# The first norm's sums from the transposed input, and the compressed branch projected first, in a hybrid decoder layer

## The chip, the cores and the metric

One core of one Trainium2 chip runs the whole layer. The metric is the device time of one execution in microseconds (us), lower is better. A profile is one further execution with the hardware profiler on; its times stand beside the plain ones.

## What is computed

One decoder layer over x, 1024 positions by 1024 channels, float32. Only the head of it matters here:

```
h  = x * rsqrt(mean(x*x, channels) + 1e-6) * norm1_g
hp = h @ w_in            # S5 channels, queries, keys and values, branch gates, merge gates
kc, vc = compress_blocks(part of hp)      # blocks of 32 positions through a small MLP
y  = merge(s5(hp), sparse_attention(hp, kc, vc))
x  = x + y @ w_out;  x = x + relu(rmsnorm(x) @ w_up)**2 @ w_down
```

The scale of the norm is one number for each position, so it can be applied behind the projection: the kernel projects x times norm1_g and multiplies the results by `rstd`, the 1024 values of rsqrt.

## The kernel before

**Layout.** x comes in transposed (`xT`, 128 channels by 1024 positions for each of eight k). Each float32 operand is split into a high part (ScalarE, ACT) and a low part (VectorE, DVE, or GpSimd, POOL), and each product is three matmuls (`mm3`, lines 76 to 78). `hTh` and `hTl` are the parts of x times norm1_g for the eight k and stay for the whole projection stage.

**u projection (lines 193 to 206).** For each k the program loads a slice of x and a block of the S5 weights `wu`, splits both, and runs 24 matmuls of 512 columns (8 x 24 = 192) into eight PSUM banks: `u0` and `u1` in the pool of two large buffers, `u2a` to `u3b` in the four small ones.

**Norm (lines 208 to 221).** In the same loop the program loads x a second time, now with positions on the partitions (sixteen tiles `xt` of 128x512), squares them on ACT with a running sum into `ss2`, and behind the loop adds the two halves and takes rsqrt in some ten small DVE steps into `rstd`. Then five DMAs in a chain, each waiting for the one before it: `rstd` goes to memory (`rD`), comes back over all partitions (`rbc`), is permuted in memory (`rsD`), repeated (`rbD`) and loaded as `rU`, the scale in the order of the S5 scan.

**Behind it.** The u banks are copied out by ACT and DVE into `uT` (two buffers) and stored to `uD`; the S5 batches load `Uc` from there and POOL multiplies it by `rU`. The token projections (`proj_tok`, tiles `pj`, 24 matmuls of 268 columns for each of eight tiles) are evicted by ACT with `rstd` (`rw`) and by DVE (`gl`). The compressed projection (`proj_cmp`, tiles `ck`, 48 matmuls of 512 columns for each of two) is evicted by DVE times `rbc` into `cT`, stored, and starts the compressed branch. The list in line 684 sets the order: `wkv0`, then the compressed `wc`, `wq0`, `wkv1`. An S5 batch runs beside them as a generator: its matrices `O1` need the powers `Pr`, `Pi` that POOL builds in a chain of small steps, and its matmuls `kp` need `AB`, which POOL adds.

**What sets the order.** A scheduler places every instruction when the program is built; on the chip each engine then runs its own list in that order, and an instruction that waits holds up all behind it. All DMAs are issued by one queue (SP). Weights pass through two raw buffers, so a third load waits until POOL or DVE has split the first.

Of the kernel before, what the change touches and what calls it, by code (L numbers as in the profile page):

```python
# [8 lines left out]
F32 = mybir.dt.float32  # L9
F32R = mybir.dt.float32r  # L10
I32 = mybir.dt.int32
AF = mybir.ActivationFunctionType
ALU = mybir.AluOpType
# [4 lines left out]
EPS = 1e-6  # L18
# [20 lines left out]
def hybrid_block(ctx: ExitStack, tc: tile.TileContext, A, out):  # L39
    nc = tc.nc  # L40
    PE, ACT, DVE, POOL, SP = nc.tensor, nc.scalar, nc.vector, nc.gpsimd, nc.sync
# [38 lines left out]
    def tt(e, o, a, b, op):  # L80
        e.tensor_tensor(out=o, in0=a, in1=b, op=op)  # L81
# [4 lines left out]
    def ts(e, o, a, s1, op0, s2=None, op1=None):  # L86
        if op1 is None:
            e.tensor_scalar(out=o, in0=a, scalar1=s1, scalar2=None, op0=op0)
        else:
            e.tensor_scalar(out=o, in0=a, scalar1=s1, scalar2=s2, op0=op0, op1=op1)  # L90
# [4 lines left out]
    def act(o, i, func=AF.Copy, **kw):  # L95
        ACT.activation(out=o, in_=i, func=func, **kw)  # L96
# [29 lines left out]
    cA = pool("cA", caas, side="right")  # L126
# [49 lines left out]
    def xtile(name):  # L176
        return xp.tile([128, 1024], F32, tag="xs", name=name)
# [4 lines left out]
    s5 = pool("s5", s5es, bufs=2)  # L182
# [6 lines left out]

    HALVES = [slice(0, 512), slice(512, 1024)]  # L190
    ss = cA.tile([128, 8], F32, name="ss")
    ss2 = cA.tile([128, 2, 8], F32, name="ss2")
    for k in range(8):
        xs = xtile("xs")
        if k:
            wh, wl = W.get("wu", A["wu"][k], DVE)
        for sl in HALVES if k == 0 else [slice(0, 1024)]:
            tc.keep_in_program_order(SP.dma_start(out=xs[:, sl], in_=A["xT"][k * 128:(k + 1) * 128, sl]))
            split_scaled(hTh[k][:, sl], hTl[k][:, sl], xs[:, sl], g1[:, k:k + 1])
            if k + sl.start == 0:  # L200
                wh, wl = W.get("wu", A["wu"][k], DVE, NP0)
        for half, m in ([(h, m) for h in range(2) for m in (2, 3, 0, 1)] if k == 0 else [(h, m) for m in (2, 3, 0, 1) for h in range(2)]):
                ms = slice(m * 128, (m + 1) * 128)
                mm3(ubank(m, half), wh[:, ms], wl[:, ms],
                    hTh[k][:, HALVES[half]], hTl[k][:, HALVES[half]], k == 0, k == 7)
        if k == 7:
            break
        for t in ((0, 1) if k == 0 else (k + 1,)):
            for hf, sl in enumerate(HALVES):
                xt = s5.tile([128, 512], F32, tag=("Ct", "St")[hf], name="xt")  # L210
                SP.dma_start(out=xt, in_=A["x"][t * 128:(t + 1) * 128, sl])
                act(xt, xt, AF.Square, accum_out=ss2[:, hf, t:t + 1])
    with tc.high_priority():
        tt(DVE, ss, ss2[:, 0], ss2[:, 1], ALU.add)
        ts(DVE, ss, ss, 1.0 / 1024, ALU.mult, EPS, ALU.add)
        rsqrt(cA, rstd, ss[:], "r1")
        SP.dma_start(out=rD[:].rearrange("(t p) -> p t", p=128), in_=rstd, allow_slow_non_contiguous=True)
        SP.dma_start(out=rbc, in_=rD[:].partition_broadcast(128))
        SP.dma_start(out=rsD[:], in_=rD[:].rearrange("(k s) -> s k", s=8), allow_slow_non_contiguous=True)
        SP.dma_start(out=rbD[:], in_=rsD[:].unsqueeze(1).to_broadcast([8, 16, 128]))  # L220
        SP.dma_start(out=rU, in_=rbD[:].rearrange("s c k -> (s c) k"))
# [139 lines left out]
    def wblock(name):  # L361
        return [W.get(name, A[name][j]) for j in range(4)]
# [317 lines left out]

    for _ in range(3):
        next(active[0])
    wa = wblock("wkv0")
    for nm, g, c0 in (("wc", 0, 256), ("wq0", None, None), ("wkv1", 0, 0), ("wm", 1, 256)):
        wn = None
        for st in proj_cmp(wa) if g is None else proj_tok(wa, g, c0):
            wn = wn or (wblock(nm) if nm != "wm" else gate_weights(0))
            bg(st)
        wa = wn
        if (g, c0) == (0, 0):  # L690
            act(gl, gl, AF.Tanh, scale=0.5)
            ts(DVE, gates, gl, 0.5, ALU.mult, 0.5, ALU.add)
            scales(0, cA, Parts(xtile("sc")))
# [3 lines left out]
    wa = wlast.pop()  # L697
# [324 lines left out]
    def T_tile(name):  # L1022
        return tmp.tile([128, 1024], F32, tag="t", bufs=3, name=name)
# [103 lines left out]
    for first_k, ms in ((0, ((0, 4, 1, 5), (0, 4, 1, 5))), (2, ((2, 6, 3, 7), (2, 3, 6, 7)))):  # L1127
        ws = {}
        for hf, order_ in zip((1, 0), ms):
            sl = HALVES[hf]  # L1130
# [39 lines left out]
    for i in range(4):  # L1170
        r = [T_tile("wo") for _ in range(2)]
# [6 lines left out]
        for c, hf in ((0, 0), (0, 1), (1, 1), (1, 0)):  # L1178
            o, sl = X2[i + 4 * c], HALVES[hf]
# [12 lines left out]
    r = [T_tile("rr") for _ in range(2)]  # L1192
# [111 lines left out]
    for j in range(1, NG - 1):  # L1304
        up(j)
        if j == 6:
            acc = {}
            for q, mo, hf in (("11", 0, 0), ("22", 4, 1), ("3", 0, 1), ("4", 4, 0)):
                acc[q] = [mlp.tile([128, 1024], F32, name=f"acc{q}{i}") for i in range(2)]
                for i in range(2):  # L1310
                    SP.dma_start(out=acc[q][i][:].rearrange("p (a t) -> p a t", a=2),
                                 in_=xD[mo + 2 * i:mo + 2 * i + 2].rearrange("a p t -> p a t")[:, :, HALVES[hf]])
# [14 lines left out]
    for p in range(7 * len(groups)):  # L1327
        g, n = groups[p // 7], ORDER[p % 7]
# [12 lines left out]
        if last and n in ("B21", "B22", "T4"):  # L1341
            a = acc[TO[n][0]]
            mo, hf = {"B21": (0, 0), "B22": (0, 1), "T4": (4, 0)}[n]
# [24 lines left out]
def layouts(inp):  # L1368
    f = {k: np.asarray(v) for k, v in inp.items()}
    x = f["x"][0]  # L1370
    w = f["w_in"][0]
    r = {}
    r["x"] = x
    r["xT"] = x.T
    r["g1"] = f["norm1_g"][0].reshape(8, 128).T

    def kblocks(cols, per):
        n = cols.shape[1]
        return cols.reshape(8 // per, per, 128, n).transpose(0, 2, 1, 3)

    perm = np.arange(512).reshape(4, 8, 16).transpose(0, 2, 1).reshape(512)
    r["wu"] = w[:, 0:512][:, perm].reshape(8, 128, 512)

    def kv(b, v, g):
        c = 1024 + ((b * 2 + v) * 2 + g) * 64
        return w[:, c:c + 64]

    gcol = w[:, 1792:1816]
    for g in range(2):
        q = w[:, 512 + g * 256:768 + g * 256]  # L1390
        kvg = np.concatenate([kv(1, 0, g), kv(2, 0, g), kv(1, 1, g), kv(2, 1, g)], axis=1)
        if g == 0:
            q = np.concatenate([q, gcol[:, :12]], axis=1)
            kvg = np.concatenate([kvg, gcol[:, 12:]], axis=1)
        r[f"wq{g}"] = kblocks(q, 2)
        r[f"wkv{g}"] = kblocks(kvg, 2)
    r["wc"] = kblocks(w[:, 1024:1280], 2)

    def dup(a):
        a = a.T  # L1400
        return np.concatenate([a, a], axis=0)

    r["a_re"] = dup(f["ssm_a_re"][0])
    r["a_im"] = dup(f["ssm_a_im"][0])
    r["log_dt"] = np.broadcast_to(f["ssm_log_dt"][0], (128, 32))
    br, bi = (f[n][0].transpose(1, 0, 2) for n in ("ssm_b_re", "ssm_b_im"))
    cr, ci = (f[n][0].transpose(2, 0, 1) for n in ("ssm_c_re", "ssm_c_im"))
    cat = lambda a, b: np.concatenate([a, b], axis=0)
    r["b1"], r["b2"], r["c1"], r["c2"] = cat(br, bi), cat(bi, br), cat(cr, ci), cat(ci, cr)
    r["dsk"] = np.broadcast_to(f["ssm_d"][0].reshape(32, 16), (16, 32, 16))  # L1410
    f32 = np.float32
    sg = np.ones((128, 2), f32)
    sg[64:, 0] = -1
    sg[:64, 1] = -1
    r["sgn"] = sg
    r["kidx"] = np.broadcast_to(np.arange(128, dtype=f32), (128, 128))
    r["gq"] = np.concatenate([f["q_norm_g"][0]] * 2)[:, None]
    r["gk"] = np.concatenate([f["k_norm_g"][0].T] * 2, axis=0)
    for c in "kv":
        r["w1" + c] = f[f"cmp_w{c}1"][0].reshape(16, 128, 128).transpose(1, 0, 2)  # L1420
        r["w2" + c] = f[f"cmp_w{c}2"][0]
        r["pe" + c] = f[f"cmp_pe_{c}"][0].reshape(16, 128).T
    p = np.arange(128)[:, None]
    d = p + 896 - np.arange(1024)[None]
    r["cbias"] = np.where(d >= 0, -d, NEG).astype(f32)
    d = p + 512 - np.arange(640)[None]
    r["wbias"] = np.where((d >= 0) & (d < 512), -d, NEG).astype(f32)
    d = p + 865 - 16 * np.arange(120)[None]
    r["mbias"] = np.where(d >= 0, -d, NEG).astype(f32)
    r["cval"] = (p >= 31).astype(f32)  # L1430
    hs = np.ones((2, 6), f32)
    for h in range(8):
        hs[h // 4, h % 4] = 0.125 / SLOPES[h]
    r["hsc"] = np.broadcast_to(hs, (128, 2, 6))
    r["bglu"] = f["ssm_b_glu"][0][perm].reshape(4, 128).T
    def mblocks(a):
        nk, nm = a.shape[0] // 128, a.shape[1] // 128
        return a.reshape(nk, 128, nm, 128).transpose(2, 1, 0, 3)

    r["wglu"] = mblocks(f["ssm_w_glu"][0][perm][:, perm])  # L1440
    r["wps"], r["wpn"] = mblocks(f["w_proj_ssm"][0][perm]), mblocks(f["w_proj_nsa"][0])
    r["wm"] = mblocks(w[:, 1816:])
    r["wo"] = mblocks(f["w_out"][0])
    r["wup"] = mblocks(f["w_up"][0])
    r["wdn"] = f["w_down"][0]
    r["g2"] = f["norm2_g"][0].reshape(8, 128).T
    r["ident"] = np.eye(128, dtype=f32)
    return {k: np.ascontiguousarray(v) for k, v in r.items()}
# [19 lines left out]
```

## Time and profile before

| | us |
|---|---|
| median of three runs | 1604.04 (1601.93 to 1607.71) |
| the profiled execution | 1599.55 |
| its span, first to last instruction | 1597.5 |
| TensorE busy | 1470.0 (92%) |
| VectorE busy | 1215.1 (76%) |
| GpSimd busy | 1031.2 (65%) |
| ScalarE busy | 706.3 (44%) |
| load of x a second time | 16 DMAs of 256 KB |

TensorE is near full over the whole span. A busy share is a mean over stages; the stage that the change touches is the first 240 us, and there its idle time lies in a few long gaps.

### The profile page before, as it was taken

How to read it: one execution, taken by the hardware profiler on the slowest of the kernel's cores; microseconds unless marked ns; L12 is line 12 of the kernel's file. 1: busy time of each engine (PE TensorE's matmuls, PEld its weight loads, DVE VectorE, ACT ScalarE, POOL GpSimd, SP SyncE). 2: the span in 40 equal slices, each digit the busy share in tenths (PEclk: the TensorE clock that was granted, in tenths of full speed). 3: DMA queues.
4: the chain of work that ended last, by engine and by line, in shares of the span. 5: the costliest groups of instructions: out<-in, count | busy, mean ns of one | idle time of the engine just before them, and what ended most of it. 6: DMA issues, size and time to landing. Idle time of an engine off the chain costs nothing.

```text
span 1597.5 us, 21469 instructions
## 1 busy us (share of the span) xinstructions
PE 1470.0 (92%) x7174; PEld 1218.0 (76%) x7174; DVE 1215.1 (76%) x1833; ACT 706.3 (44%) x1443; POOL 1031.2 (65%) x875
## 2 busy tenths in 40 slices
PE   8599899999988999998788868999999889999999
PEld 6488788788977888887566756888888667787877
DVE  6366887521278878976798998977778999998965
ACT  6143433321277878887545542222222244343431
POOL 2565466442055546553688967988888766989883
PEclk9799999999989999999898979999999989999999
DMA  8654523352211111112935225332232341323202
GB/s 283 87 158 117 152 83 106 106 182 93 76 34 45 59 57 53 37 54 72 356 106 185 92 86 192 139 112 106 106 111 92 107 144 67 132 82 125 77 1 105
DMA packets 111680, 174.86 MB, mean 109 GB/s; under 512 B 23489, under 2 KB 44737, under 8 KB 111570
## 3 DMA queue, kind: packets, MB, share of 16 engines
q1 hardware_dynamic: 111570, 173.49, 33.4%
q8 instruction: 57, 0.93, 0.2%
q14 instruction: 53, 0.43, 0.1%
HBM read 125.20 MB, written 46.22 MB: 107 GB/s over the span
## 4 chain that ended last, share of the span: by engine, by line
PE 30%; DVE 12%; DMA 4%; POOL 3%; issue 3%; ACT 0%; SPq 0%; DVEq 0%; POOLq 0%; ACTq 0%
PE wT L76 3%; PE wT L77 3%; PE wT L78 3%; PE wB L76 2%; PE wB L78 2%; PE wB L77 2%; PE dn L78 2%; PE dn L76 2%; PE dn L77 2%; POOL wl L81 2%; DVE rr L81 2%; PE dnc L76 1%; PE dnb L78 1%; PE dnc L77 1%; PE dnc L78 1%
## 5 line engine op out<-in xcount | busy, mean ns | idle before, releaser
L81 POOL TENSOR_TENSOR wl<-raw,wh 128x512 fp32r<-128x512 f32 x132 | 196.7, 1500 | 85.8 <-ACT wh L96 85.5
L81 POOL TENSOR_TENSOR wl<-wd,wh 128x512 fp32r<-128x512 f32 x96 | 147.2, 1542 | 61.6 <-ACT wh L96 61.2
L96 ACT ACTIVATE wh<-raw 128x512 fp32r<-128x512 f32 x132 | 82.2, 628 | 159.8 <-PE wB L77 81.4
L90 POOL TENSOR_SCALAR pS<-pS,rs 128x128 f32<-128x128 f32 (+7 forms) x64 | 48.2, 754 | 105.6 <-DVE rs L81 69.0
L96 ACT ACTIVATE wh<-wd 128x512 fp32r<-128x512 f32 x96 | 59.2, 625 | 103.6 <-POOL wd L81 41.7
L81 DVE TENSOR_TENSOR pl<-ptp,ph 128x512 fp32r<-128x512 f32 x132 | 88.3, 686 | 18.6 <-ACT ph L96 17.4
L76 PE MATMUL gt<-hTh,wmh 128*128 128x512 f32 x256 | 101.6, 397 | 0.0
L77 PE MATMUL gt<-hTl,wmh 128*128 128x512 f32 x256 | 101.3, 396 | 0.0
L78 PE MATMUL gt<-hTh,wml 128*128 128x512 f32 x256 | 101.2, 395 | 0.0
L81 POOL TENSOR_TENSOR wl<-sum,wh 128x512 fp32r<-128x512 f32 x56 | 89.3, 1597 | 17.6 <-ACT wh L96 17.6
L96 ACT ACTIVATE ph<-ptp 128x512 fp32r<-128x512 f32 (+1 forms) x148 | 83.9, 589 | 13.7 <-PE ptp L898 11.8
L81 DVE TENSOR_TENSOR rr<-rr,rs 128x512 f32<-128x512 f32 x64 | 88.3, 1388 | 1.8
L81 POOL TENSOR_TENSOR wd<-wd 128x512 f32<-128x512 f32 x48 | 76.6, 1600 | 2.9 <-PE dnb L77 1.0
L96 ACT ACTIVATE wh<-sum 128x512 fp32r<-128x512 f32 x56 | 35.1, 628 | 92.3 <-PE wT L77 29.5
L81 DVE TENSOR_TENSOR rr<-wT,rr 128x512 f32<-128x512 f32 x80 | 54.7, 686 | 27.3 <-PE wT L78 26.7
L81 DVE TENSOR_TENSOR gt<-gt,rbc 128x512 f32<-128x512 f32 x32 | 22.0, 688 | 68.3 <-PE gt L78 61.7
L93 DVE SCALAR_TENSOR_TENSOR rr<-rr 128x512 f32<-128x512 f32 x64 | 70.5, 1107 | 1.8
L96 ACT ACTIVATE pW<-pW,mx 128x64 f32<-128x64 f32 (+5 forms) x128 | 65.4, 515 | 7.2 <-DVE mx L853 6.7
L90 POOL TENSOR_SCALAR pW<-pW,rs 128x64 f32<-128x64 f32 (+5 forms) x128 | 67.2, 538 | 0.0
L889 PE MATMUL op<-ph,vs 128*128 128x512 f32 x132 | 61.2, 464 | 2.0 <-DVE ot L81 1.4
L853 DVE CUSTOM_DVE_ANT_0 pS<-sS,c_cbias 128x128 f32<-128x128 f32 (+7 forms) x64 | 48.1, 752 | 19.5 <-PE sS L819 16.4
L81 POOL TENSOR_TENSOR wml<-wmr,wmh 128x512 fp32r<-128x512 f32 x32 | 43.5, 1364 | 25.8 <-ACT wmh L96 25.6
(638 smaller groups left out, 5233.7 us busy)
## 6 DMA issues: line engine op xcount, KB each, us to landing
raw<-in_wup SPq DMA_DIRECT2D x68, 256.0 KB, 2.6
wd<-in_wdn SPq DMA_DIRECT2D x64, 256.0 KB, 2.9
hD<-rr SPq DMA_DIRECT2D x26, 512.0 KB, 2.7
ru<-hD SPq DMA_DIRECT2D x18, 512.0 KB, 3.9
wmr<-in_wm SPq DMA_DIRECT2D x32, 256.0 KB, 2.9
gD<-gt SPq DMA_DIRECT2D x32, 256.0 KB, 2.1
g<-gD SPq DMA_DIRECT2D x32, 256.0 KB, 5.4
raw<-in_wo SPq DMA_DIRECT2D x20, 256.0 KB, 3.3
```

The source lines that it names most:

```text
L76: PE.matmul(out=o, lhsT=lh, rhs=rh, start=first, stop=False)
L77: PE.matmul(out=o, lhsT=lh, rhs=rl, start=False, stop=False)
L78: PE.matmul(out=o, lhsT=ll, rhs=rh, start=False, stop=last)
L81: e.tensor_tensor(out=o, in0=a, in1=b, op=op)
L90: e.tensor_scalar(out=o, in0=a, scalar1=s1, scalar2=s2, op0=op0, op1=op1)
L93: DVE.scalar_tensor_tensor(out=o, in0=a, scalar=s, in1=b, op0=op0, op1=op1)
L96: ACT.activation(out=o, in_=i, func=func, **kw)
L853: DVE.tensor_tensor_reduce(out=dst, in0=ps, in1=bias, scale=nsl, scalar=3e38, op0=ALU.add, op1=ALU.min, accum_out=mx[:, b, h:h + 1])
L889: PE.matmul(out=op, lhsT=vv, rhs=ph, start=n == 0, stop=n == len(jobs) - 1)
```

## The change

The second load of x goes, with its squares and `ss2`. In its place ACT squares the halves of the slices of x that are there already, POOL adds them up over k into `ssqT` and `ssqUc` (128 channels by 512 positions each; 14 additions), and behind the loop eight matmuls of one column with a column of ones sum over the partitions into a PSUM tile `ssp`, position on the partition, from which DVE takes the mean. The compressed projection moves to the head of the list, ahead of `wkv0`.

```diff
@@ u projection and norm
-    ss2 = cA.tile([128, 2, 8], F32, name="ss2")
+    ssq = [s5.tile([128, 512], F32, tag=t, name="ssq" + t) for t in ("T", "Uc")]
+    one = cA.tile([128, 1], F32, name="one")
+    DVE.memset(one, 1.0)
...
-        if k == 7:
-            break
-        for t in ((0, 1) if k == 0 else (k + 1,)):
-            for hf, sl in enumerate(HALVES):
+        for hf, sl in enumerate(HALVES):
+            if k == 0:
+                act(ssq[hf], xs[:, sl], AF.Square)
+            else:
                 xt = s5.tile([128, 512], F32, tag=("Ct", "St")[hf], name="xt")
-                SP.dma_start(out=xt, in_=A["x"][t * 128:(t + 1) * 128, sl])
-                act(xt, xt, AF.Square, accum_out=ss2[:, hf, t:t + 1])
+                act(xt, xs[:, sl], AF.Square)
+                tt(POOL, ssq[hf], ssq[hf], xt, ALU.add)
     with tc.high_priority():
-        tt(DVE, ss, ss2[:, 0], ss2[:, 1], ALU.add)
-        ts(DVE, ss, ss, 1.0 / 1024, ALU.mult, EPS, ALU.add)
+        sps = B_tile("ssp", (128, 8))
+        for t in range(8):
+            PE.matmul(out=sps[:, t:t + 1], lhsT=ssq[t // 4][:, t % 4 * 128:(t % 4 + 1) * 128], rhs=one, start=True, stop=True)
+        ts(DVE, ss, sps, 1.0 / 1024, ALU.mult, EPS, ALU.add)
@@ order of the projections
-    wa = wblock("wkv0")
-    for nm, g, c0 in (("wc", 0, 256), ("wq0", None, None), ("wkv1", 0, 0), ("wm", 1, 256)):
+    wa = wblock("wc")
+    for nm, g, c0 in (("wkv0", None, None), ("wq0", 0, 256), ("wkv1", 0, 0), ("wm", 1, 256)):
```

The scheduler places everything anew up to the middle of the attention. The list of the DMA queue SP before, from the last slice of x on (out<-in, partitions by elements; `wcr`, `wkv0r` and `wq0r` are raw weights):

```order
L198 DMA xs<-in_xT 128x1024
L142 DMA wkv0r<-in_wkv 128x536 x3
L217 DMA rD<-rstd 128x8x1
L142 DMA wkv0r<-in_wkv 128x536
L218 DMA rbc<-rD 128x1024
L219 DMA rsD<-rD 1024x1x1
L357 DMA uD<-uT 128x8x128
L220 DMA rbD<-rsD 128x1x128
L142 DMA wcr<-in_wc 128x512
L357 DMA uD<-uT 128x8x128
L142 DMA wcr<-in_wc 128x512
L221 DMA rU<-rbD 128x128
```

And the same queue in the changed kernel, from the weights that follow the last slice of x:

```order
L142 DMA wcr<-in_wc 128x512 x4
L142 DMA wkv0r<-in_wkv 128x536 x4
L361 DMA uD<-uT 128x8x128
L142 DMA wq0r<-in_wq 128x536
L361 DMA uD<-uT 128x8x128 x2
L142 DMA wq0r<-in_wq 128x536
L361 DMA uD<-uT 128x8x128
L544 DMA Uc<-uD 128x512 x2
L221 DMA rD<-rstd 128x8x1
L222 DMA rbc<-rD 128x1024
L223 DMA rsD<-rD 1024x1x1
L224 DMA rbD<-rsD 128x1x128
```

All eight raw weights, the four stores of u and the two loads of `Uc` now stand ahead of the chain from `rD` on.

VectorE before, from the first step of the norm to `rstd`, which stand among the splits of the last two k:

```order
L81 TENSOR_TENSOR ss<-ss_140 128x8
L90 TENSOR_SCALAR ss<-ss 128x8
L88 TENSOR_SCALAR r1i<-ss 128x8
...
L93 SCALAR_TENSOR_TENSOR hTl_115<-xs,c_g_66,hTh_107 128x1024
L81 TENSOR_TENSOR O_694<-c_c_499,Pr 128x576
L81 TENSOR_TENSOR r1t<-r1i 128x8
L81 TENSOR_TENSOR O_1059<-c_c_499,Pr 128x576
L93 SCALAR_TENSOR_TENSOR r1t<-r1t,ss 128x8
L93 SCALAR_TENSOR_TENSOR rstd<-r1t,r1i 128x8
L81 TENSOR_TENSOR p3b<-c_c_501,Pi 128x576
```

VectorE in the changed kernel, from the first copy of u to the first step of the norm:

```order
L360 COPY uT<-u2b 128x8x64
L81 TENSOR_TENSOR O_701<-c_c_506,Pr 128x576
L81 TENSOR_TENSOR O_954<-c_c_506,Pr 128x576
L360 COPY uT<-u3b 128x8x64
L360 COPY uT<-u_133 128x8x64
L81 TENSOR_TENSOR p3b<-c_c_508,Pi 128x576
L81 TENSOR_TENSOR O_701<-O_701,p3b 128x576
L90 TENSOR_SCALAR ss<-ssp 128x8
L360 COPY uT<-u_134 128x8x64
L88 TENSOR_SCALAR r1i<-ss 128x8
```

The norm's steps now stand behind the copies of u and behind steps that read POOL's `Pr` and `Pi`.

On POOL the first S5 batch stands so in the changed kernel:

```order
L81 TENSOR_TENSOR p1a<-c_b_502,Fr 128x512
L81 TENSOR_TENSOR p2a<-c_b_504,Fi 128x512
L81 TENSOR_TENSOR Uc<-Uc,rU 128x512 x2
L81 TENSOR_TENSOR AB<-p1a,p2a 128x512
L578 MEMSET sa 128x4
```

As before, `AB` stands behind two products with `rU`. On TensorE the matmuls `kp` that read `AB` stood behind 143 matmuls `pj`; now they stand behind 12 `pj`, 48 `ck` and 58 more `pj`.

## Rows read from the trace of the kernel before

**Rows 1.** The page: its first line.
```profile
span 1597.5 us, 21469 instructions
```

**Rows 2.** Stretches: length, busy time (count) by engine, granted TensorE clock, DMA share, GB/s.
```profile
54.95:96.60 41.65, 22.06 (x144) 21.20 (x142) 9.27 (x21) 9.95 (x21) 17.49 (x17) 0.71 0.73 139
83.15:86.67 3.52, 3.52 (x16) 3.52 (x16) 2.15 (x4) 2.25 (x6) 2.30 (x3) 0.50 0.91 265
86.67:96.60 9.93, 9.93 (x81) 9.82 (x80) 3.22 (x10) 3.48 (x8) 7.18 (x7) 0.99 0.53 181
96.60:240.00 143.40, 133.04 (x853) 120.14 (x853) 107.99 (x183) 59.09 (x109) 79.16 (x69) 0.98 0.41 116
```

**Rows 3.** Timeline of TensorE: start, duration, work, [idle before it, who ended it].
```profile
54.55 0.40 PE L78 MATMUL u<-hTh,wul 128*128 128x512 f32 x1
...
64.22 0.59 PE L374 MATMUL pj<-wkv0h,hTh 128*128 128x268 f32 x1 [7.01 <-ACT wkv0h L96]
...
83.15 0.59 PE L374 MATMUL pj<-wkv0h,hTh 128*128 128x268 f32 x1 [11.97 <-DVE gl L88]
...
96.63 1.05 PE L547 MATMUL kp<-O,AB 128*16 128x128 f32 x8
...
105.04 0.39 PE L76 MATMUL ck<-hTh,wch 128*128 128x512 f32 x1
105.27 0.39 PE L77 MATMUL ck<-hTl,wch 128*128 128x512 f32 x1
```

**Rows 4.** DMA issues up to 200 us: count, size of one, us from issue to landing.
```profile
rU<-rbD SPq DMA_DIRECT2D x1, 64.0 KB, 3.7
...
rD<-rstd SPq DMA_DIRECT2D x1, 4.0 KB, 11.6
```

**Rows 5.** Timeline of the DMA queue SP: when each DMA was issued.
```profile
50.94 0.39 SPq L217 DMA_DIRECT2D rD<-rstd  x1
52.22 0.34 SPq L142 DMA_DIRECT2D wkv0r<-in_wkv  x1
62.51 0.33 SPq L218 DMA_DIRECT2D rbc<-rD  x1
62.88 0.82 SPq L219 DMA_DIRECT2D rsD<-rD  x1
75.65 0.68 SPq L220 DMA_DIRECT2D rbD<-rsD  x1
...
78.09 1.06 SPq L221 DMA_DIRECT2D rU<-rbD  x1
```

**Rows 6.** Groups by shape, TensorE, 0 to 120 us: idle before, who ended it.
```profile
L77 PE MATMUL u2a<-hTl,wuh 128*128 128x512 f32 x8 | 3.6, 449 | 1.3 <-DVE hTl L93 1.3
```

**Rows 7.** Timeline of GpSimd.
```profile
34.23 1.04 POOL L81 TENSOR_TENSOR Ct<-c_kidx,fl 128x512 f32<-128x512 f32 x1 [3.90 <-DVE c_pek L81]
...
38.19 2.04 POOL L81 TENSOR_TENSOR Ct<-c_kidx,fl 128x512 f32<-128x512 f32 x1
...
49.12 1.36 POOL L81 TENSOR_TENSOR wkv0l<-wkv0r,wkv0h 128x536 fp32r<-128x536 f32 x1
50.44 0.46 POOL L81 TENSOR_TENSOR Pi<-cx,cx 128x128 f32<-128x128 f32 x1
...
93.34 1.29 POOL L81 TENSOR_TENSOR AB<-p1a,p2a 128x512 f32<-128x512 f32 x1
```

**Rows 8.** Timeline of VectorE.
```profile
38.05 1.27 DVE L93 SCALAR_TENSOR_TENSOR hTl<-xs,c_g,hTh 128x1024 fp32r<-128x1024 f32 x1
...
48.76 0.17 DVE L93 SCALAR_TENSOR_TENSOR rstd<-r1t,r1i 128x8 f32<-128x8 f32 x1
...
52.84 0.79 DVE L81 TENSOR_TENSOR O<-O,p3b 128x576 f32<-128x576 f32 x1
```

**Rows 9.** Who TensorE waited for, 96 to 240 us: total, times, longest.
```profile
PE pj L374 <- DVE gl L88: 2.6, 2, 2.0
```

**Rows 10.** A stretch at the start of the attention (columns as in rows 2).
```profile
440.00:460.00 20.00, 15.43 (x81) 14.07 (x80) 15.81 (x70) 13.81 (x50) 9.41 (x17) 0.66 0.10 29
```

More of the change, by code (lines that the diff above doesn't have):

```diff
@@ L1372, in layouts @@
     r = {}
-    r["x"] = x
     r["xT"] = x.T
```

## Prediction

> **What bounds the kernel now.** The page first: TensorE is busy for nine tenths of the 1597.5 us span [rows 1], so a change gains what idle or slowly clocked TensorE time it removes, and loses what it adds. Next the stretches of the head. From the end of the u matmuls at 54.95 to the first S5 matmul `kp` at 96.63 TensorE works 22.06 of 41.65 us, at a mean clock of 0.71 [rows 2]. The timeline names the two gaps: 7.01 us for the last block of `wkv0`, and 11.97 us put down to `gl` [rows 3]. The queue of DMAs shows what stands behind both. `rD`, 4 KB, holds the DMA engines for 11.6 us [rows 4]; the last `wkv0` load was issued behind it at 52.22 and landed only after it. `rsD`, of the same 1024 single values, holds them for 12.8 us (62.88 to 75.65), and the stores of u queue behind that [rows 5]. ACT, which copies u, waits for a store, and its evictions of `pj` stand behind the copy. So the head is bound by two slow scattered DMAs in front of weights and stores. Neither gap comes from the second load of x.
>
> The work in that stretch: 143 matmuls `pj`. At the upper clock 81 of them take 9.93 us [rows 2], 0.1226 us each, so 17.5 us of work in 41.7: 24.2 us are lost.
>
> **The change part by part.**
>
> *The load of x goes.* 16 DMAs of 256 KB, and 16 accumulated squares on ACT become 16 plain squares. In the u loop TensorE waited 1.3 us for operands that came late [rows 6], so at most that is gained there, and u ends at 53.6 or later.
>
> *14 additions on POOL.* 1.29 us each by the like `AB` [rows 7], 18 us in all; 12 of them lie beside POOL's idle time before 34.23, where it waited 3.90 us for DVE [rows 7]. Not free are those that stand ahead of the powers. The chain of powers ran from 34.23 to 50.90, 16.7 us, with one weight split in it. Now the last two additions (2.6), four splits of `wc` (5.2) and two more of `wkv0` (1.36 each, 2.7) lie in it: 10.5 us more. The chain can begin when the additions of the seventh k are done: I estimate this, from 12 x 1.29 and the constants that POOL prepares and waits for beside them, at about 34, as before. So `Pi` is done near 61. Bounds: 57 if it runs without the collisions seen before (below), 64 if each weight's round through the two raw buffers is waited for.
>
> *The eight matmuls of one column.* No row shows such a matmul on a float32 operand; `kp`, eight records of 128 columns, takes 1.05 us [rows 3], so 0.1 to 1.1 us. They stand where TensorE has a wait right behind, and cost nothing; without that wait, 1 us.
>
> *The norm's steps on DVE.* Before, they stood among the splits of the last k, and `rstd` was ready at 48.9 [rows 8]. Now the order puts them behind `p3b` and `O1`, which read `Pi`. From `Pi` at 61: `p3b` and `O1` 0.8 each [rows 8], and by estimate 0.2 for `ss`, 0.7 (as `O1`, near its size) for a copy of u that also waits for a store, and 3.0 for eleven dependent steps between 0.17 [rows 8] and twice that: `rstd` at about 66.5, 17.6 us later than before. Bounds 62.5 and 72.
>
> *The chain of DMAs.* It is unchanged, so its length is read from the issue times: `rD` 11.57 until `rbc`, 0.37, `rsD` 12.77, `rbD` 2.44 [rows 5], `rU` 3.7 [rows 4], 30.9 us. Then two products with `rU` and `AB` on POOL, 3.9 us [rows 7]. So `kp` cannot start before `rstd` + 35, that is 101.5. Before, the stores and loads of u came behind the chain and `kp` came 47.7 behind `rstd`; now they are ahead of it, which shortens that to 35 but does not make up for 17.6.
>
> *What TensorE does until then.* The order puts 48 `ck` (0.233 each by the spacing in rows 3, 11.2 us) and 70 `pj` (8.6) ahead of `kp`: 19.8 us of work, 2.3 more than before. It has three waits in it. The first `ck` needs the bank of `u0`, whose copy on DVE stands behind `Pr`: about 58 to 60. The third `pj` needs `gl`, behind `cT`, which waits for `rbc` (`rstd` + 16, about 82 to 83). And `kp` waits for `AB`. The weights are hidden: all eight loads now stand ahead of `rD`. That removes the 7.01.
>
> *The sum.* At `kp`: 101.5 - 96.63 = 4.9 later, less 2.3 of work done earlier, 2.6. After a gap of 7 or 12 us the granted clock was 0.50 for some microseconds: 16 `pj` took 3.52 instead of 1.96 us [rows 2], so 1.6 more, and 2.4 behind the 7 us gap by the same reckoning. Before, `kp` began at the upper clock [rows 2]; now it begins after a long wait: 2.0. Together +4.6, say +5. The gain of the first part is inside this, since `kp` is set by `rU`, not by the end of u. From 96.6 to 240 TensorE idled 10.4 us in seven small waits [rows 2, 9]; the same kinds of waits stand in the new order, so I leave them as they are. The profiled execution would take 1599.55 + 5 = 1604.6. The median of the runs lay 4.5 above that execution, so I say 1609.
>
> With `rstd` as the one unknown: the time is even at `rstd` near 62, and each microsecond later costs one.
>
> **A rule against the change.** The first additions of like shape on POOL took 1.29 [rows 7], and the two-input DVE step `O1` on 576 elements 0.79 [rows 8]. The Trainium skill, GPSIMD Engine Reference, section Engine selection, says to put elementwise additions on VectorE since GpSimd is about twice as slow for two inputs. The trace agrees (0.79 for 576 elements against 1.29 for 512). By the rule the additions on DVE would end the sums about 1 us earlier after the last square; the sum above does not change by more.
>
> **The rivals.**
>
> *The norm comes early (faster).* If the powers and the copies do not hold up DVE, `rstd` comes at about 52, soon behind the u matmuls, as the change intends: then `kp` comes at 87, the whole scattered chain lies behind 20 us of work, and the sum is 14.5 us better than the forecast: 1594 to 1595. It decides at `rstd` before 57 for a gain beyond 0.3%. For it: the squares themselves can be ready by 40. Against it: the order is fixed, and the steps stand behind `Pi`.
>
> *The compressed branch first removes later waits.* Its chain (`cD`, `ct`, `hps`) starts one stage earlier, so the 10.4 us of waits up to 240 [rows 2], among them 2.6 for `gl` [rows 9], could fall to 2: 8 us, net -3, 1601. Against it: `gl` waits come from DVE's order, and the new order has a product that waits for a store in it.
>
> *Collisions on the way to `Pi` (slower still).* `Ct` on POOL took 1.04 alone and 2.04 where it began 0.14 us behind a DVE step of 1.27 [rows 7, 8]: it waited for it. Six to eight more such meetings, 1 us each, put `rstd` at 73 to 74: +12, 1616. The Trainium skill, SBUF — State Buffer, section SBUF: two separate sides, calls the port pair of DVE and GpSimd an exclusive lock held for a whole instruction; by that rule each of the 14 additions can meet a split. The trace agrees with the 2.04. Against it: most additions lie ahead of the chain, with slack.
>
> *The attention is placed anew* up to about 560 us. TensorE idles 4.6 of 20 us there, with a clock of 0.66 [rows 10]; another order of the same steps may give or take 4 us. It has no sign and widens the range.
>
> **How the numbers follow.** Forecast, `rstd` between 62 and 72, +0 to +10: 0.60, of which 0.34 lies beyond +0.3% (4.8 us, about what a measurement of this kernel can tell from no change) and 0.26 within. The early norm: 0.12, faster. Later waits gone: 0.16, of which 0.11 within and 0.05 faster. Collisions: 0.12, slower. Faster 0.17, same 0.37, slower 0.46. The forecast's own range is 1604 to 1614; with 4 us for the attention, the collisions and the second rival, 1598 to 1620; left out are the early norm and the ends of the others.
>
> **What would show it.** No `xt` load. `rstd` near 66 and `rD` right behind it. The eight weights issued ahead of `rD` and no wait for them on TensorE. A wait of some 3 to 6 us before the first `ck`, of 7 to 10 put down to `gl` behind `rbc`, and of 12 to 14 for `AB` before `kp` at 101 to 102. It would be wrong if `rstd` came before 57, if `kp` did not wait for `rU`, or if the waits of TensorE between `kp` and the gate projection differ by more than 5 us from 10.4.

## The result and the profile after

The changed kernel takes 1621.98 us in the median of four runs (1620.10 to 1622.49); the kernel before took 1604.46 in the same comparison (1601.93 to 1607.71). The ratio is 1.0094, with a 95% interval of 1.0073 to 1.0114: slower by some 15 us (the two medians lie 17.5 apart). The direction was forecast, and the size was three times the +5 of the sum. By the ratio the 1604.04 of the prediction would become 1619: beyond its own 1604 to 1614, at the upper end of its wide range, 1598 to 1620.

The first line of the page of the changed kernel, which answers to [rows 1]: 22.2 us more between the two profiled executions. (That of the kernel before, 1599.55, lay below the four runs of this comparison, so the size is read from the ratio.)

```profile
span 1619.7 us, 21488 instructions
```

TensorE's timeline of the changed kernel (start, length, work, then in brackets the idle time before it and who ended it) answers to [rows 3, 6]:

```profile
29.95 0.80 PE L77 MATMUL u2a<-hTl,wuh 128*128 128x512 f32 x1 [4.85 <-DVE hTl L93]
...
59.41 0.39 PE L78 MATMUL u<-hTh,wul 128*128 128x512 f32 x1
63.02 1.02 PE L218 MATMUL ssp<-one,ssqT 128*128 128x1 f32 x8 [3.22 <-ACT uT L96]
...
66.33 0.59 PE L378 MATMUL pj<-wkv0h,hTh 128*128 128x268 f32 x1 [1.31 <-ACT uT L96]
...
69.96 0.80 PE L76 MATMUL ck<-hTh,wch 128*128 128x512 f32 x1 [0.59 <-DVE uT L360]
...
93.72 0.59 PE L378 MATMUL pj<-wkv0h,hTh 128*128 128x268 f32 x1 [5.62 <-DVE gl L88]
...
114.97 1.89 PE L551 MATMUL kp<-O,AB 128*16 128x128 f32 x8 [15.98 <-POOL sa L578]
```

The wait of 7.01 for `wkv0h` is gone, as meant. But the u matmuls end at 59.8 instead of 54.95, and `kp` starts at 114.97 instead of 96.63, 18.3 us later. (`sa`, put down as its releaser, is a small memset right behind `AB` on GpSimd.) By the last gate matmul the lag is 22.2 us, and it is 22.2 at the end: the loss is made in the head.

VectorE's timeline of the changed kernel answers to [rows 8]; the last row is `rstd`:

```profile
15.03 1.28 DVE L93 SCALAR_TENSOR_TENSOR e_r<-e_n,e_r 128x32 f32<-128x32 f32 x1
...
20.33 3.27 DVE L93 SCALAR_TENSOR_TENSOR e_p<-e_p,e_r 128x32 f32<-128x32 f32 x4
23.64 3.62 DVE L93 SCALAR_TENSOR_TENSOR dt<-e_p,e_i 128x32 f32<-128x32 f32 x1
...
28.62 1.28 DVE L93 SCALAR_TENSOR_TENSOR hTl<-xs,c_g,hTh 128x1024 fp32r<-128x1024 f32 x1
...
36.78 1.28 DVE L93 SCALAR_TENSOR_TENSOR hTl<-xs,c_g,hTh 128x1024 fp32r<-128x1024 f32 x1 [2.67 <-ACT hTh L96]
37.98 1.29 DVE L93 SCALAR_TENSOR_TENSOR em<-em 128x32 f32<-128x32 f32 x1
...
39.30 1.28 DVE L93 SCALAR_TENSOR_TENSOR em<-em 128x32 f32<-128x32 f32 x1
40.51 1.83 DVE L81 TENSOR_TENSOR wul<-wur,wuh 128x512 fp32r<-128x512 f32 x1
42.26 1.28 DVE L90 TENSOR_SCALAR fh<-e_r 128x32 f32<-128x32 f32 x1
...
77.51 0.17 DVE L93 SCALAR_TENSOR_TENSOR rstd<-r1t,r1i 128x8 f32<-128x8 f32 x1
```

The steps `e_p` and `dt` on VectorE in the kernel before:

```profile
20.70 1.32 DVE L93 SCALAR_TENSOR_TENSOR e_p<-e_p,e_r 128x32 f32<-128x32 f32 x6
22.06 0.19 DVE L93 SCALAR_TENSOR_TENSOR dt<-e_p,e_i 128x32 f32<-128x32 f32 x1
```

GpSimd's timeline of the changed kernel: additions over the same time, the start of the chain of powers and its end:

```profile
14.45 1.81 POOL L81 TENSOR_TENSOR ssqT<-ssqT,xt 128x512 f32<-128x512 f32 x1
16.23 1.29 POOL L81 TENSOR_TENSOR ssqUc<-ssqUc,xt 128x512 f32<-128x512 f32 x1
...
22.21 1.30 POOL L81 TENSOR_TENSOR ssqT<-ssqT,xt 128x512 f32<-128x512 f32 x1
23.49 1.28 POOL L81 TENSOR_TENSOR ssqUc<-ssqUc,xt 128x512 f32<-128x512 f32 x1
24.74 1.26 POOL L81 TENSOR_TENSOR ssqT<-ssqT,xt 128x512 f32<-128x512 f32 x1
25.96 1.25 POOL L81 TENSOR_TENSOR ssqUc<-ssqUc,xt 128x512 f32<-128x512 f32 x1
37.41 1.81 POOL L81 TENSOR_TENSOR ssqT<-ssqT,xt 128x512 f32<-128x512 f32 x1 [10.20 <-ACT xt L96]
...
41.74 1.75 POOL L81 TENSOR_TENSOR ssqUc<-ssqUc,xt 128x512 f32<-128x512 f32 x1
...
47.10 0.24 POOL L81 TENSOR_TENSOR cx<-Pi 128x32 f32<-128x32 f32 x1 [0.23 <-DVE Pi L81]
...
69.12 0.46 POOL L81 TENSOR_TENSOR Pi<-cx,cx 128x128 f32<-128x128 f32 x1
```

Here the additions show what they cost. Six `e_p` steps of 32 elements took 1.32 us together before; now four of them take 3.27, and `dt` takes 3.62 instead of 0.19. It begins inside the second of four additions that follow each other without a gap, and ends at 27.26, with the last of them (27.21). It is not always so: `e_r`, begun at 15.03, ends at 16.31, where one addition ends (16.26) and the next begins (16.23). Who goes first is not shown.

Behind `dt` in VectorE's order stands `hTl` of the fourth k, at 28.62. TensorE waits 4.85 us for it, up to 29.95, and its granted clock is low from there on (length, busy time and count by engine PE, PEld, DVE, ACT and POOL, then the granted clock, the DMA share and GB/s):

```profile
29.95:34.30 4.35, 4.34 (x11) 3.44 (x12) 4.16 (x21) 0.87 (x3) 0.00 (x0) 0.54 0.59 178
```

At a mean of 0.54, close to the lower level (0.50, 1.2 GHz), these 4.35 us lose some 2.0 more. Together this is 6.9 us; in the kernel with the additions on VectorE (below) the u matmuls end 7.4 us earlier than here.

The constants behind `dt` are 2.7 us late at first (`e_n` at 33.93, at 31.27 before). Then VectorE waits 2.67 us for the next `hTh`, and the next four additions, from 37.41 to 43.49, stretch four of its steps by about 1.1 us each (the rows from 37.98 on). So the powers start at 47.1 (35.5 before) and `Pi` is done at 69.6 (50.9).

The DMA queue SP of the changed kernel answers to [rows 5]:

```profile
77.70 0.37 SPq L221 DMA_DIRECT2D rD<-rstd  x1
88.40 0.32 SPq L222 DMA_DIRECT2D rbc<-rD  x1
88.78 0.81 SPq L223 DMA_DIRECT2D rsD<-rD  x1
104.98 0.65 SPq L224 DMA_DIRECT2D rbD<-rsD  x1
109.42 0.33 SPq L225 DMA_DIRECT2D rU<-rbD  x1
```

Up to the issue of `rU` the chain takes 31.7 us, 4.6 more than before: `rD` 10.7 us, `rsD` 16.2 (12.8 before), `rbD` 4.4 (2.4 before).

### The profile page after: what moved, and what is told of

Its sections match the earlier page's. It is cut to its first block, busy times and chain, and to the rows that moved or that the text cites. A ratio compares the mean times of both kernels' runs of the same rounds, so it can differ in the third digit from the quotient of the medians.

```text
span 1619.7 us, 21488 instructions
## 1 busy us (share of the span) xinstructions
PE 1478.4 (91%) x7190; PEld 1224.9 (76%) x7190; DVE 1224.6 (76%) x1833; ACT 704.4 (43%) x1427; POOL 1044.9 (65%) x889
## 4 chain that ended last, share of the span: by engine, by line
PE 29%; DVE 13%; POOL 3%; issue 3%; DMA 2%; ACT 1%; SPq 0%; DVEq 0%; POOLq 0%; ACTq 0%
PE wT L76 3%; PE wT L77 3%; PE wT L78 3%; PE wB L76 2%; PE wB L78 2%; PE wB L77 2%; PE dn L78 2%; PE dn L76 2%; PE dn L77 2%; DVE rr L81 2%; DVE acc L81 1%; POOL wl L81 1%; PE dnc L76 1%; PE dnb L78 1%; DVE T3l L81 1%
## 5 line engine op out<-in xcount | busy, mean ns | idle before, releaser
L81 DVE TENSOR_TENSOR pl<-ptp,ph 128x512 fp32r<-128x512 f32 x132 | 88.1, 685 | 11.5 <-ACT ph L96 10.3
L90 POOL TENSOR_SCALAR pW<-pW,rs 128x64 f32<-128x64 f32 (+5 forms) x128 | 67.9, 543 | 0.0
L893 PE MATMUL op<-ph,vs 128*128 128x512 f32 x132 | 61.2, 464 | 2.0 <-DVE ot L81 1.4
L895 PE MATMUL op<-pl,vs 128*128 128x512 f32 x132 | 56.1, 425 | 3.6 <-DVE pl L81 3.2
```

The lines of the kernel that those rows point to most:

```text
L893: PE.matmul(out=op, lhsT=vv, rhs=ph, start=n == 0, stop=n == len(jobs) - 1)
L895: PE.matmul(out=op, lhsT=vv, rhs=pl, start=False, stop=False)
```

## The experiments

Theory A: the additions on GpSimd hold up VectorE, so `rstd` is late, and `kp` follows `rstd` through the chain of DMAs. Rival B: the new order of the projections costs the time. Rival C: the norm is late because it stands behind the powers in VectorE's order. A last question (rival D) is whether the scattered DMAs bound the head at all.

**Only the norm** (`norm_only`: the projections in the old order):

```diff
-    wa = wblock("wc")
-    for nm, g, c0 in (("wkv0", None, None), ("wq0", 0, 256), ("wkv1", 0, 0), ("wm", 1, 256)):
+    wa = wblock("wkv0")
+    for nm, g, c0 in (("wc", 0, 256), ("wq0", None, None), ("wkv1", 0, 0), ("wm", 1, 256)):
```

> The changed kernel with the first norm from the transposed input and the additions on GpSimd, but with the projections in the order of the kernel before (wkv0 first). Theory A (the additions hold up VectorE, so the constants, the powers and rstd are late, and kp with them): rstd at 75 to 80 as in the changed kernel (77.5), kp at 110 to 116, a time 12 to 20 us above the kernel before. Rival B (the order of the projections costs the time: the matmuls ck wait, and the third pj waits for cT): with the old order the time is back within 4 us of the kernel before, whatever rstd does.

Ratio 1.0097 (1.0070 to 1.0124); `rstd` at 78.9, `kp` at 112.7. The norm alone costs what the whole change costs, so B does not explain the changed kernel.

**Only the order** (`cmp_only`: the same lines the other way round, in the kernel before):

> The kernel before with only the order of the projections changed (compressed branch first); x is loaded a second time, no additions on GpSimd. Theory A: rstd at 48 to 55 as in the kernel before, the eight weights or most of them ahead of rD, kp no later than 97, a time between 10 us below and 2 us above the kernel before. Rival B: 10 to 17 us above the kernel before, with the waits for gl behind cT and for AB.

1.0052 (1.0033 to 1.0072), some 8 us: neither theory's figure. `rstd` comes at 48.3 and `kp` at 97.0, as before, but the two gaps of 7 and 12 us have become one. VectorE and TensorE in this kernel, one row each:

```profile
77.84 0.69 DVE L356 COPY uT<-u 128x512 f32<-128x512 f32 x1 [23.77 <-ACT uT L96]
```

```profile
78.58 0.80 PE L76 MATMUL ck<-hTh,wch 128*128 128x512 f32 x1 [24.30 <-DVE uT L356]
```

The first `ck` needs the bank of `u0`, and the copy out of it waits, through its buffer, for a store of u that was issued at 63.45, while the scattered `rsD` (62.52 to 76.22) was under way. From 100 to 425 us TensorE idles 17.0 us, against 11.5 before.

**The additions on VectorE (`dve_adds`), and no additions at all (`no_adds`, without the line):**

```diff
-                tt(POOL, ssq[hf], ssq[hf], xt, ALU.add)
+                tt(DVE, ssq[hf], ssq[hf], xt, ALU.add)
```

> The changed kernel with the 14 additions on VectorE in place of GpSimd. Theory A: no VectorE step of 32 elements takes more than 0.3 us before 30 us, and the wait of 4.85 us for hTl at 29.95 is gone, so the u matmuls end near 54 to 55. VectorE carries 14 x 0.69 = 9.7 us more, and its order puts the last of the constants behind the splits of the last k, so the powers start at about 48 to 50 all the same; rstd at 68 to 74, a time 4 to 10 us below the changed kernel. Rival B: within 3 us of the changed kernel.

> The changed kernel without the 14 additions: the sums of squares hold only the first eighth of the input, which leaves the norm wrong and the rest of the work as it is. Theory A: short VectorE steps are short again, the u matmuls end at 53.5 to 55, the powers start at 34 to 36 and not at 47, rstd at 62 to 68 and kp at 98 to 105: 10 to 16 us below the changed kernel, that is 1604 to 1610 beside 1604 before. Rival B: within 3 us of the changed kernel. Rival C (the norm's place in VectorE's order behind the powers is enough by itself): rstd does not come before 62 here either, and the time stays at or above that of the kernel before.

On VectorE: 1.0004 (0.9990 to 1.0018), no change against the kernel before, and 14 us below the changed kernel, more than theory A had said. The u matmuls end at 52.4, `rstd` comes at 68.6 and `kp` at 104.7. The powers start at 47.1, as late as in the changed kernel, but `Pi` is done at 61.6. That no short step is stretched before 30 us did not come true: five `e_p` steps that meet GpSimd's products for the constants take 2.97 us there, one of them 1.24. Without additions: 1.0031 (1.0016 to 1.0045). The powers start at 34.4 and `Pi` is done at 54.2, but `rstd` still comes at 67.8. VectorE in that kernel shows why:

```profile
55.03 0.79 DVE L81 TENSOR_TENSOR O<-O,p3b 128x576 f32<-128x576 f32 x1
...
61.14 0.69 DVE L359 COPY uT<-u 128x512 f32<-128x512 f32 x1 [4.12 <-ACT uT L96]
61.75 0.15 DVE L90 TENSOR_SCALAR ss<-ssp 128x8 f32<-128x8 f32 x1
...
67.59 0.17 DVE L93 SCALAR_TENSOR_TENSOR rstd<-r1t,r1i 128x8 f32<-128x8 f32 x1
```

The norm stands behind a copy of u that waits for a store, and shares its eleven steps with other work. So A and C both hold in part: the additions on GpSimd make up 9 to 10 us of the changed kernel's `rstd` (77.7 against 68.6 and 67.8). Of these, 2.6 can be the last two additions' own time in the chain of powers. Of the rest the norm's place is 10.7, by `norm_early` below.

In the kernel without additions `kp` comes at 76.8, not at 98 to 105 as expected. `AB` stands ahead of the products with `rU` there, so TensorE waits for these at its next matmuls, which start 30.0 us behind `rstd`:

```profile
97.76 2.08 PE L566 MATMUL xx<-Uc,I 128*128 128x128 f32 x8 [13.25 <-POOL Uc L81]
```

Why this kernel takes some 4 us more than the one with the additions on VectorE (the intervals just meet) is not shown.

**The additions alone** (`pool14`: in the kernel before; nobody reads the sums):

```diff
+    acc = [s5.tile([128, 512], F32, tag=t, name="acc" + t) for t in ("T", "Uc")]
...
+        for hf, sl in enumerate(HALVES):
+            if k == 0:
+                POOL.memset(acc[hf], 0.0)
+            else:
+                tt(POOL, acc[hf], acc[hf], xs[:, sl], ALU.add)
```

> The kernel before with 14 additions of 128x512 on GpSimd, placed in the u loop as in the changed kernel (each half of the transposed input is added to an accumulator that nobody reads); the norm still comes from the second load of x, and stands ahead of O and p3b in VectorE's order. Theory A (the additions hold up VectorE and with it the constants and the powers, whatever the norm does): short VectorE steps of over 1 us between 10 and 45 us, the powers start at 42 to 48 instead of 35.5, Pi ends at 62 to 70; rstd at 52 to 58, so 5 to 12 us above the kernel before. Rival C (the additions cost only because the norm stands behind Pi): within 3 us of the kernel before, although Pi is late.

1.0046 (1.0030 to 1.0062), 7 us, although the norm's own steps are where they were. `rstd` comes at 56.6. Steps of 32 elements take over 1 us again (VectorE):

```profile
29.32 1.27 DVE L93 SCALAR_TENSOR_TENSOR th<-e_n,th 128x32 f32<-128x32 f32 x1
30.51 0.18 DVE L93 SCALAR_TENSOR_TENSOR em<-em,e_r 128x32 f32<-128x32 f32 x1
30.62 1.26 DVE L90 TENSOR_SCALAR th<-th 128x32 f32<-128x32 f32 x1
```

The powers start at 38.6, not at 42 or later, and `Pi` is done at 94.4, not at 62 to 70, so there the expectation missed; the delay comes in the u loop, which ends at 65.2. (Part of that is not contention: the additions read the slices and keep their buffers longer.) The last two loads of `wkv0` then stand behind `rsD`, and TensorE waits 16.0 us for `wkv0h` instead of 7.0 (GpSimd waits 23.4 for it, in the midst of the powers). With that reservation it speaks against rival C alone: additions cost here with the norm in its old place.

**The additions on VectorE and the old order (`dve_tok`):**

> The kernel before with the first norm from the transposed input, the additions on VectorE, and the projections in the old order. If the order of the projections is worth nothing once rstd is late (as norm_only and the changed kernel say, 1.0097 and 1.0094): rstd at 67 to 70, kp at 102 to 106, within 4 us of dve_adds, 1599 to 1606. If the compressed branch first costs 8 us here too, as in cmp_only: 1592 to 1596.

1.0037 (1.0018 to 1.0056); `rstd` 68.6, `kp` 103.5. About 5 us above the same kernel with the compressed branch first, so here the new order helps a little (the intervals just meet), which neither branch of the expectation had; with the additions on GpSimd it made no difference (`norm_only`).

**The norm early** (`norm_early`: additions on VectorE; `after` is one and `c` unchanged, but both are worked out from `rstd`, so that the steps have to stand behind it):

```diff
+    for c in (C1, C2):
+        stt(c[:, 0, 0:1], rstd[:, 0:1], 0.0, c[:, 0, 0:1], ALU.mult, ALU.add)
...
+    stt(after, rstd[:, 0:1], 0.0, one, ALU.mult, ALU.add)
...
-                DVE.tensor_copy(out=dst, in_=src)
+                if m < 2:
+                    ts(DVE, dst, src, after[:, 0:1], ALU.mult)
```

> dve_adds with the products O, p3b and two copies of u made to wait for rstd (a factor of one and a sum with zero, both worked out from rstd), so that the norm stands ahead of them in VectorE's order. The prediction's rule that kp follows rstd, with break-even at rstd near 62: rstd at 57 to 60 instead of 68.5, kp at 94 to 100, 4 to 10 us below dve_adds, 1592 to 1598. If instead something else ends last once the norm is early (the stores and loads of u, which now stand behind rsD again): kp at 100 to 106 and a time within 3 us of dve_adds.

0.9978 (0.9963 to 0.9994), 4 us below `dve_adds`, the low end of the expectation. `rstd` comes at 57.9, 10.7 earlier, but `kp` only 4.2 earlier, at 100.5, where the second branch of the expectation had it. Its DMA queue:

```profile
60.64 0.43 SPq L221 DMA_DIRECT2D rD<-rstd  x1
69.53 0.33 SPq L222 DMA_DIRECT2D rbc<-rD  x1
69.91 0.82 SPq L223 DMA_DIRECT2D rsD<-rD  x1
...
74.56 0.37 SPq L368 DMA_DIRECT2D uD<-uT  x1
...
87.28 0.69 SPq L224 DMA_DIRECT2D rbD<-rsD  x1
```

`rD` goes out 2.7 us behind `rstd`, since a load of weights stands ahead of it in the queue and is issued at 60.26, and `rsD`, with a store of u beside it, takes 17.4 us. The chain gives back over half of what the earlier `rstd` gains.

**The chain made on the chip.** The five DMAs are replaced in the kernel before (`chip_before`), in the changed kernel (`chip_after`), in the one with additions on VectorE (`chip_dve`), and in the one with only the order changed (`chip_cmp`). `msk` is worked out once from the identity; the removed DMAs and the lines for `ident`, `ones` and `msk` are left out:

```diff
+        for hf, sl in enumerate(HALVES):
+            dg = s5.tile([128, 512], F32, tag="zz", name="dg")
+            mul(DVE, dg[:].rearrange("p (a b) -> p a b", b=128), ident[:, None, :].to_broadcast([128, 4, 128]), rstd[:, 4 * hf:4 * hf + 4, None].to_broadcast([128, 4, 128]))
+            rps = B_tile("rps")
+            PE.matmul(out=rps, lhsT=ones, rhs=dg, start=True, stop=True)
+            act(rbc[:, sl], rps)
+        for hf, sl in enumerate(HALVES):
+            dm = s5.tile([128, 512], F32, tag="zz", name="dm")
+            dv = dm[:].rearrange("p (k s) -> p k s", s=8)
+            mul(DVE, dv, rbc[:, sl].rearrange("p (k s) -> p k s", s=8), msk[:, None, :].to_broadcast([128, 64, 8]))
+            DVE.tensor_reduce(out=rU[:, 64 * hf:64 * hf + 64], in_=dv, axis=AX.X, op=ALU.add)
```

> The kernel before with rbc and rU made on the chip: rstd times the identity (VectorE), two matmuls with a matrix of ones, two copies by ScalarE, and for rU a product with a mask and a sum over eight. The five DMAs rD, rbc, rsD, rbD, rU are gone. Theory A (the two scattered DMAs and what queues behind them bound the head): no wait of 7.0 for wkv0h and none of 12.0 for gl; kp at 73 to 80 instead of 96.6, the work before it 2 us less; 14 to 20 us below the kernel before, 1583 to 1589. Rival D (the loss in the head is made by the weights and stores themselves and would come back as other waits): kp after 88, less than 8 us below.

> The changed kernel with rbc and rU made on the chip, the additions on GpSimd kept. Theory A: rstd stays near 76 to 79 (collisions and order unchanged), but kp follows it by 10 to 14 us instead of 37, so at 87 to 92: 18 to 25 us below the changed kernel, 1596 to 1604. Rival D: kp after 100, less than 10 us below.

> The changed kernel with rbc and rU made on the chip and the additions on VectorE: both suspected costs gone. Theory A: rstd at 66 to 70, kp at 78 to 84, 1582 to 1591. If the collisions are a cause on their own, the difference to chip_after is 8 to 16 us.

> The kernel before with rbc and rU made on the chip and the compressed branch projected first; x is loaded a second time. Theory A on the 24.3 us wait of the first ck in cmp_only (the bank of u0 is freed by a copy that waits for a store of u, and the store lies behind rsD): without the scattered DMAs this wait is 2 to 9 us, and the time lies within 5 us of chip_before. Rival B (the compressed branch first costs 8 us by itself): 6 to 12 us above chip_before.

The kernel before with it: 0.9904 (0.9881 to 0.9928), 15 us faster, the best of all. Its TensorE:

```profile
57.81 1.13 PE L226 MATMUL rps<-dg,ones 128*128 128x512 f32 x2 [0.64 <-ACT uT L96]
62.48 0.59 PE L384 MATMUL pj<-wkv0h,hTh 128*128 128x268 f32 x1 [3.55 <-ACT rbc L96]
...
80.78 1.05 PE L557 MATMUL kp<-O,AB 128*16 128x128 f32 x8
```

Both long gaps are gone (3.55 us are left, for `rbc`), and `kp` is no longer waited for. The changed kernel with it: 0.9978 (0.9967 to 0.9988), 19 us below the changed kernel, with `rstd` still at 77.0 and `kp` 14 behind it, at 91.0. With that rival D falls.

The other two missed. With additions on VectorE `kp` comes at 80.8, 10 us earlier than in the changed kernel with the chain made on the chip, yet the time is the same: 0.9985 (0.9970 to 0.9999). The last token matmul of TensorE in the one with additions on GpSimd and in the other:

```profile
443.40 0.28 PE L390 MATMUL pj<-wq1l,hTh 128*128 128x256 f32 x1
```

```profile
436.74 0.28 PE L390 MATMUL pj<-wq1l,hTh 128*128 128x256 f32 x1
```

6.7 us are left there; at the last matmul of the attention it is 1.4 (754.5 and 753.1). So the 14 us that the additions on GpSimd cost are shown only with the chain of DMAs in place. With only the order changed, the wait of the first `ck` falls from 24.3 to 2.0, as theory A said, but the time is 0.9970 (0.9958 to 0.9982), 11 us above the best one, as rival B said: from 100 to 425 us TensorE idles 18.6 us, against 11.6.

**All of it, in the old order** (`chip_early`: norm from the transposed input, additions on VectorE, norm early, chain on the chip):

> The first norm from the transposed input with everything cured that the runs so far blame: additions on VectorE, the norm ahead of O, p3b and two copies of u, rbc and rU made on the chip, and the projections in the old order. If these are all the costs, what is left is what the missing load of x is worth: u matmuls end at 52 to 53 (chip_before 56.1), rstd at 57 to 58, a wait of 5 to 6 us before the two matmuls with ones, kp at 77 to 80 (80.8), so 0 to 4 us below chip_before: 1584 to 1588. If the norm from the transposed input has a further cost that is not named yet: 1590 or more.

0.9922 (0.9893 to 0.9950): not to be told from the best one. The u matmuls end at 53.9 (56.1 there), `rstd` comes at 60.5 and `kp` at 84.3, later than expected. So the 0 to 4 us below `chip_before` are not shown. With the known costs cured as far as here, the missing load of x is worth nothing that shows; with `rstd` still 10.5 us later than there, what it is worth by itself stays open.

| kernel | time to before | u ends | `rstd` done | `kp` | `wq1` ends | rest |
|---|---|---|---|---|---|---|
| before | 1 | 55.0 | 48.9 | 96.6 | 441.2 | 1156.3 |
| changed | 1.0094 | 59.8 | 77.7 | 115.0 | 463.4 | 1156.3 |
| norm_only | 1.0097 | 61.2 | 78.9 | 112.7 | 459.6 | 1157.0 |
| cmp_only | 1.0052 | 54.3 | 48.3 | 97.0 | 451.4 | 1158.1 |
| dve_adds | 1.0004 | 52.4 | 68.6 | 104.7 | 446.1 | 1152.4 |
| no_adds | 1.0031 | 52.3 | 67.8 | 76.8 | 451.7 | 1153.9 |
| pool14 | 1.0046 | 65.2 | 56.6 | 118.6 | 454.4 | 1155.3 |
| dve_tok | 1.0037 | 52.7 | 68.6 | 103.5 | 448.5 | 1158.0 |
| norm_early | 0.9978 | 52.4 | 57.9 | 100.5 | 442.6 | 1152.9 |
| chip_before | 0.9904 | 56.1 | 50.0 | 80.8 | 429.2 | 1158.8 |
| chip_after | 0.9978 | 60.5 | 77.0 | 91.0 | 443.7 | 1151.0 |
| chip_dve | 0.9985 | 53.2 | 67.9 | 80.8 | 437.0 | 1162.6 |
| chip_cmp | 0.9970 | 55.4 | 49.3 | 77.6 | 434.3 | 1160.6 |
| chip_early | 0.9922 | 53.9 | 60.5 | 84.3 | 430.9 | 1155.9 |

Times in us from one profiled execution of each; `kp` is the start of the first one; "`wq1` ends" is the last matmul of the token projection behind the gates, "rest" is the span less the end of the last `wq1` matmul.

## Why the prediction was right in its sign and short in its size

**What bounds the head** was right: the scattered DMAs. Taking them out is worth 15 us to the kernel before and 19 to the changed one.

**The load of x** was mis-sized, and with the wrong sign. The sum took the additions as a cost to GpSimd alone and let u end at 53.6; it ended at 59.8, by the gap of 4.85 us before 29.95 and the low clock behind it. With the additions on VectorE it ends at 52.4, so the step would have held without the additions on GpSimd.

**The additions on POOL** is the step that failed. It said that the powers begin at about 34 "as before", because GpSimd had the time for 12 additions beside its idle time. GpSimd had; VectorE had not. Its constants were late, and the additions of the seventh k, which had to wait for their inputs, were done only at 43.5. So the powers began at 47.1 (with the `Ct` from which the prediction counted 34.23, at 45.3) and ended at 69.6, outside the bounds of 57 to 64. Their length was not short: 24.3 us from that `Ct`, against 27 in the sum.

The late start alone is not the price. With the additions on VectorE the powers start at 47.1 too, but they take 14.5 us instead of 22.5, with the splits of `wc` ahead of them and no additions in them, and the u matmuls end 7.4 us earlier.

The rival on collisions had the mechanism and the row for it, and came nearest (`rstd` at 73 to 74 and +12, with a chance of 0.12; measured 77.7 and some +15). But it counted meetings only on the way to `Pi` and set against it that most additions lie ahead of the chain. Those were the costly ones. The SBUF page of the Trainium skill (SBUF — State Buffer, section SBUF: two separate sides) calls the port pair of the two engines an exclusive lock held for a whole instruction. The trace bears that out with steps that end with an addition (1.28 for `e_r`), and at 23.64 shows a case beyond it: a step did not get in between three successive additions.

**The rule against the change**, weighed and set aside there (the Trainium skill, GPSIMD Engine Reference, section Engine selection: elementwise additions belong on VectorE), was judged by the length of the additions, "about 1 us". By `dve_adds` it was worth 14 us, since the other engine pays too; with the chain made on the chip it was worth nothing that shows.

**The eight matmuls of one column** took 1.02 us, within the 0.1 to 1.1.

**The norm's steps on DVE**: `rstd` was to come 5.5 us behind `Pi`, at 66.5. In the changed kernel it comes 8.1 behind `Pi`, at 77.7, beyond the bound of 72. That the two kernels without additions on GpSimd have it at 67.8 and 68.6 is luck. Without additions `Pi` is done at 54.2, and `rstd` comes 13.6 behind it. In both the first step of the norm stands behind the copy of u that waits for a store (to 61.14 and 58.76), with the additions on VectorE even ahead of `p3b`. The copy was named there, at 0.7 us and without the wait.

**The chain of DMAs**: `kp` at `rstd` + 35 held: 37.3 in the changed kernel, 33.9 to 36.1 in the three with the same chain, the u stores ahead of it and `kp` behind it. It does not hold in `norm_early` (42.6), where `rD` is issued late and `rsD` is longer. Of the +18.3 at `kp`, the forecast's +4.9 lacked 11.2 for `rstd` and 2.3 for the chain.

**What TensorE does until then**: the sizes of the waits were near, though outside their ranges (for `gl` 5.6, forecast 7 to 10; for `AB` 16.0, forecast 12 to 14), and the wait before the first `ck` had moved ahead to `ssp` and `pj` (3.2 and 1.3; 0.6 was left at `ck`). The clock behind the longest wait, answering to [rows 2] (columns as above):

```profile
59.80:114.95 55.15, 28.46 (x134) 24.86 (x134) 15.27 (x28) 7.99 (x15) 22.09 (x36) 0.73 0.38 105
114.95:119.26 4.31, 4.29 (x19) 3.50 (x20) 4.08 (x9) 1.76 (x4) 0.38 (x2) 0.50 0.57 140
```

The granted clock of 0.50 is the lower level, 1.2 GHz, for 4.3 us; the 2.0 of the sum was of that size.

**The rivals.** The early norm did not come, since `rstd` came after 57. That the compressed branch first removes later waits is refuted: the idle time of TensorE from `kp` to the end of the gate projection is 13.4 us, 11.5 before, and where the order alone is changed it is 5 to 7 us more. That the attention is placed anew was right in kind and too narrow in size: in the table the rest of the program takes 1151 to 1163 us, with no plain relation to the head. Part of that is the spread of single executions: those of the kernel before lie between 1595.9 and 1608.8. Why the rest is long in one build and short in another stays open; it may hide what the additions cost in the two kernels with the chain made on the chip.

Not explained either is why `rsD` took 16.2 us in the changed kernel and 17.4 in `norm_early`, and 12.1 to 13.7 in the seven others: a store of u beside it is no rule, since `cmp_only` and the kernel before had one too (13.7 and 12.8), and the changed kernel had none.

## What to carry to other kernels

Work that moves to an idle engine is not free if that engine shares a way to the operands with a busy one: look at what the busy engine does in the same microseconds, and above all at its short steps, which here waited for whole instructions of the other. Read from the built order what a moved step stands behind, before reckoning with when its inputs are ready. And where a small vector has to go from partitions to all partitions, count the microseconds of its scattered DMAs and of what queues behind them: here a multiplication with the identity and a matmul with ones brought the first user from 37 to 14 us behind the vector.

## What the runs showed of the hardware

A VectorE step of 32 elements, 0.19 us alone, took 3.62 us (in the changed kernel and in `norm_only`) while GpSimd additions of 1.3 us ran without a gap, and ended with the last of them; single meetings cost about 1.1 us each (1.27 for `th` in `pool14`).

A DMA of 1024 single values of four bytes took 8.9 to 11.9 us to write `rD` and 12.1 to 17.4 to permute `rsD`, and a load or store issued behind it waited for its end. The page DMA: Bandwidth & Descriptors of the Trainium skill, section Rules for kernel authors, says that a non-contiguous last dimension becomes one descriptor for each element and should be avoided. The runs agree: the kernel before has 2112 packets under 512 bytes more than the same kernel with the chain made on the chip (23489 and 21377), twice the 1024 values and 64, and a chain with two such DMAs costs 15 us in 1600.
